# Prompt attention of a hybrid decoder: the diagonal mask moves into the scan, the heads' bias into the score products

## The chip, the cores and the metric

The kernel runs on one core of one Trainium2 chip. The metric is device time in microseconds of one execution of the whole program. Five engines work on it at the same time: TensorE (PE; its weight loads, PEld, run beside its matmuls), VectorE (DVE), ScalarE (ACT), GpSimd (POOL) and SyncE (SP), which here does nothing but issue DMAs. Each engine takes its own instructions in a fixed order and waits on semaphores for the others.

## The reference, cut to what matters

One layer of a decoder, for a prompt of 2048 tokens and a small sample group. The change touches the stick-breaking attention of the prompt alone: 8 heads of 64 channels, strictly causal.

```python
def sb_block(q, k, v, bias, q_pos, k_pos):
    z = (jnp.einsum('nqhd,nkhd->nhqk', q, k).astype(jnp.float32) * (SB_HEAD_DIM ** -0.5)
         + bias.astype(jnp.float32)[None, :, None, None])
    mask = (k_pos[None, :] < q_pos[:, None])[None, None]
    log_beta = jax.nn.log_sigmoid(z)
    log_1m = jnp.where(mask, jax.nn.log_sigmoid(-z), 0.0)
    rc = lax.cumsum(log_1m, axis=3, reverse=True)
    a = jnp.exp(jnp.where(mask, log_beta + rc - log_1m, -jnp.inf))
    return jnp.einsum('nhqk,nkhd->nqhd', a.astype(v.dtype), v)
```

For one query, the weight of key k is sigmoid(z_k) times the product of sigmoid(-z_j) over the later keys j that are still before the query. The rest of the layer (input projections, a convolution, a pooling mixer, cross-attention to a memory, the sample group's attention over a paged cache, the output projection with two norms) is as it was.

## The kernel before

The program has three stretches that follow one another on TensorE: the input projections with the sample group's paged attention beside them (to about 1486 us), the prompt's stick-breaking attention (1486 to about 1965 us), and the output projection (to the end). Everything below is about the middle one, `sb_prompt`.

**Order of the work.** The loop runs over blocks `(hp, qb)`: 4 pairs of heads, and for each 4 blocks of 512 queries. Inside a block it runs over key chunks `kc` of 512 keys from the diagonal (`kc == qb`) down to 0, and inside a chunk over 4 *steps*: query tiles `q2` = 0 and 2 (two tiles of 128 queries at a time) times the two heads `hh` of the pair. There are 40 chunks and 160 steps. TensorE's order is the order in which the program is written; the other engines' orders are set by a scheduler. A list `late` delays parts of a step: its transposes are written four steps after its scores (`TURN`), its products with the values seven steps after (`SUM` more). So while the scores of a chunk are made, the transposes belong to the chunk before it.

**One step**, with the names that the profile uses:
- `sb_scores` (L1271): 4 matmuls into `S` (PSUM, 2 buffers). Queries and keys are split into a high and a low part of fp32r. The key tile `kT` holds the high part on 64 partitions and the low part on the other 64; the query tile `Q` holds the high part (twice) and the low part (twice). Two products of depth 128 are added up.
- `sb_gates` (L1275, L1276): two sigmoids on ACT out of `S`, `gam` = sigmoid(-z) and `be` = sigmoid(z). The head's bias enters here, as an operand with one value per partition (`nbias_bc`, `bias_bc`).
- the scan (L1342 on the diagonal, L1345 else) on DVE: a running product of `gam` from the last key down, into `E`. On the diagonal it starts from 1 and `ZM` holds ones above the diagonal, so that masked keys leave the product at 1.
- the multiply (L1354) on POOL: `be` times `E`, in place.
- `turn`, four steps later: TensorE transposes the 128x128 pieces of `be` (L1373) into `AT` (PSUM, 2 buffers), three or four pieces to a tile. A full tile of 4 pieces is copied to `at` by ACT (L1378). A tile with a diagonal piece has 3 pieces (384 columns); DVE brings it out, and multiplies by a mask `tri` (L1376).
- `values`, seven steps later: products of `at` with `V`, added up in `av` (L1388). At the end of a block DVE multiplies `av` by the gate `sgt` into `sbo` (L1393), and SP stores that.

```python
                if n < 512:
                    dve.tensor_tensor(out=at[:, :n], in0=ap_[:, :n], in1=tri, op=ALU.mult)
                else:
                    act.copy(at, ap_)
```

**Loads.** `load(hp, qb)` issues 8 DMAs on SP: for each head two for `kT` (L1254) and two for `Q` (L1255). `Q` has 4 buffers, two blocks' worth, `kT` has 10. The first two blocks, (0, 0) and (0, 1), are loaded by `sb_early` before the attention stretch begins; it also makes the first two steps' scores. Side work (sums of the output weights on POOL, L1599, the end of the sample group, the head of the convolution's norm) is interleaved by step count.

Of the kernel before, what the change touches and what calls it, by code (L numbers as in the profile page):

```python
# [8 lines left out]
F32 = mybir.dt.float32  # L9
# [9 lines left out]
P = 128  # L19
# [47 lines left out]
BEB = 6  # L67
# [25 lines left out]
def kernel(  # L93
# [50 lines left out]
    mvd = dram.tile([4, P, 2, 2 * P], F32, name="mvd")  # L144
    c11d = dram.tile([8, P, 512], F32, name="c11d")
# [40 lines left out]
    nbias_bc = con.tile([P, NH], F32, name="nbias_bc")  # L186
# [250 lines left out]
    def mem_rows(mp, ps, c):  # L437
# [13 lines left out]
        if c >= 4:  # L451
            split2(mp, nat.rearrange("p t n -> p (t n)"), cc, mvd, f"v{cc}")

# [787 lines left out]
    def sb_loader(sbr):  # L1241
# [3 lines left out]
        def load(hp, qb):  # L1245
            tok = slice(512 * qb, 512 * qb + 512)
            Q = []
            for hh in range(2):
                pr = slice(64 * hh, 64 * hh + 64)
                kt = sbr.tile([P, 512], F32R, tag="kT", name=f"kT{hp}_{qb}_{hh}", bufs=10)  # L1250
                qt_ = sbr.tile([P, 2, 512], F32R, tag="Q", name=f"Q{hp}_{qb}_{hh}", bufs=4)
                for x in range(2):
                    hx = slice(64 * x, 64 * x + 64)
                    sp.dma_start(kt[hx].bitcast(F32), kd[hp, pr, x, tok])  # L1254
                    sp.dma_start(qt_[hx].bitcast(F32), qd[hp, pr, :, tok])  # L1255
                KT[hp, hh, qb] = kt
# [11 lines left out]
    def sb_scores(S, h, q2, w, Q, kt):  # L1268
        for j in range(2):
            for x in range(2):  # L1270
                pe.matmul(S[:, j, :w], lhsT=Q[:, x, P * (q2 + j) : P * (q2 + j + 1)], rhs=kt[:, :w], start=x == 0,  # L1271
                          stop=x == 1)

    def sb_gates(S, h, w, ga, be):
        act.activation(out=ga, in_=S[:, :, :w], func=AF.Sigmoid, bias=nbias_bc[:, h : h + 1], scale=-1.0)  # L1275
        act.activation(out=be, in_=S[:, :, :w], func=AF.Sigmoid, bias=bias_bc[:, h : h + 1])  # L1276

    def sb_early(load, blk, sbr, bps, early):

        room = sbr.tile([P, 16, P], F32, tag="V", name="early", bufs=2).rearrange("p (n j b) c -> p n j (b c)", n=4, j=2)  # L1280
        for n in range(2):
            blk[0, n] = load(0, n)
        for _ in range(3):
            yield
        for hh in range(2):
            S = bps.tile([P, 512], F32, tag="AT", name=f"Se{hh}", bufs=2).rearrange("p (j k) -> p j k", j=2)
            Q, KT, _ = blk[0, 0]
            sb_scores(S, hh, 0, 2 * P, Q[hh], KT[0, hh, 0])
            early[hh] = room[:, 2 * hh], room[:, 2 * hh + 1]
            sb_gates(S, hh, 2 * P, *early[hh])  # L1290
            yield

    def sb_prompt(load, loaded, sb, bps, ops, zmp, early, values_of, flags, newest):


        zm = sb.tile([P, 512], F32, tag="sbo", name="zm", bufs=1)
        pool.memset(zm, 0.0)
        pool.affine_select(out=zm[:, 384:512], in_=zm[:, 384:512], compare_op=ALU.is_gt, fill=1.0, base=0,
                           pattern=[[-1, P]], channel_multiplier=1)
        ZM = zmp.tile([P, 512], F32, name="ZM", bufs=1)  # L1300
        act.copy(ZM, zm)
        tri = sb.tile([P, 384], F32, name="tri", bufs=1)
        pool.memset(tri, 1.0)
        for c in (0, 256):
# [99 lines left out]
        for bi, (hp, qb) in enumerate(blocks):  # L1404
            if bi == 0:
                values_of(0)
# [779 lines left out]
```

## Time and profile before

| what | value |
|---|---|
| time, median of 3 runs | 2383.82 us (2381.51 to 2388.36) |
| the profiled execution's own time | 2395.19 us |
| its span, first to last instruction | 2393.5 us |
| mean granted TensorE clock | 0.987 |
| PE busy over the span | 2266.5 us |
| attention stretch, 1486 to 1970 us | PE busy 420.25, ACT 420.39, DVE 374.69, POOL 376.25 of 484 us |

Busy time is read as follows: an engine is busy from an instruction's start to its end, and overlapping instructions count once. "Idle before <- X" in a row of the profile is the idle time of the engine just before those instructions, and X is what ended it. Times of a chunk below run from the start of its first gate on ACT to the start of the next chunk's.

### The profile page before, as it was taken

How to read it: one execution, taken by the hardware profiler on the slowest of the kernel's cores; microseconds unless marked ns; L12 is line 12 of the kernel's file. 1: busy time of each engine (PE TensorE's matmuls, PEld its weight loads, DVE VectorE, ACT ScalarE, POOL GpSimd, SP SyncE). 2: the span in 40 equal slices, each digit the busy share in tenths (PEclk: the TensorE clock that was granted, in tenths of full speed). 3: DMA queues.
4: the chain of work that ended last, by engine and by line, in shares of the span. 5: the costliest groups of instructions: out<-in, count | busy, mean ns of one | idle time of the engine just before them, and what ended most of it. 6: DMA issues, size and time to landing. Idle time of an engine off the chain costs nothing. (4 is left out here: it accounts for less than half of the span.)

```text
span 2393.5 us, 43149 instructions
## 1 busy us (share of the span) xinstructions
PE 2266.5 (95%) x16512; PEld 1817.6 (76%) x16512; DVE 1686.7 (70%) x2308; ACT 1133.7 (47%) x1967; POOL 1297.7 (54%) x1348
## 2 busy tenths in 40 slices
PE   7989999999999999999999998898988889999997
PEld 7888888888888777777777776666666668787775
DVE  5332785969657674577777877878787775676997
ACT  5322243242442322224242425798989885444553
POOL 3544545555565546445556453687887773532333
PEclk9999999999999999999999999899999999999999
DMA  6678977878778999888877876564544307876774
GB/s 208 199 263 290 346 260 253 290 247 291 241 263 308 319 348 344 309 287 276 298 261 267 265 253 158 131 175 145 155 110 117 87 10 218 275 222 193 247 249 146
DMA packets 336871, 557.99 MB, mean 233 GB/s; under 512 B 27985, under 2 KB 212433, under 8 KB 320266
## 3 DMA queue, kind: packets, MB, share of 16 engines
q1 hardware_dynamic: 281290, 286.53, 39.1%
q0 software_dynamic: 55376, 268.72, 31.6%
q8 instruction: 130, 2.13, 0.4%
q14 instruction: 75, 0.61, 0.1%
HBM read 465.09 MB, written 90.68 MB: 232 GB/s over the span
## 5 line engine op out<-in xcount | busy, mean ns | idle before, releaser
L975 DVE STREAM_TRANSPOSE T<-kt 128x1024 f32<-128x1024 f32 x256 | 308.6, 1226 | 188.9 <-PE sSA L988 172.3
L942 POOL DMA_INDIRECT vt<-in_cache_v_dram,idv x256 | 252.4, 986 | 254.8 <-PE sO L1027 194.0
L627 DVE SCALAR_TENSOR_TENSOR cacc<-U,par,cacc 128x512 f32<-128x512 f32 x480 | 359.7, 749 | 11.0
L1354 POOL TENSOR_TENSOR be<-be,E 128x512 f32<-128x512 f32 (+4 forms) x316 | 301.9, 963 | 94.6 <-DVE E L1342 46.9
L1345 DVE TENSOR_TENSOR_SCAN E<-gam,cr,ZM 128x513 f32<-128x513 f32 x192 | 234.2, 1265 | 35.4 <-ACT gam L1275 30.9
L942 POOL DMA_INDIRECT kt<-in_cache_k_dram,idk x128 | 128.2, 1002 | 199.2 <-DVE T L975 156.5
L1373 PE MATMUL AT<-ident,be 128*128 128x128 f32 x1082 | 159.1, 283 | 52.5 <-DVE at L1376 36.5
L1373 PEld LDWEIGHTS AT<-ident,be 128*128 128x128 f32 x1082 | 120.3, 143 | 101.4 <-DVE at L1376 43.7
L2005 PE MATMUL acc<-wohi,mh 128*128 128x512 f32 (+1 forms) x480 | 192.3, 401 | 1.2 <-ACT mh L1729 1.1
L2005 PE MATMUL acc<-wolo,mh 128*128 128x512 f32 (+1 forms) x480 | 188.9, 393 | 0.7 <-DVE wolo L1640 0.7
L1275 ACT ACTIVATE gam<-S,nbias_bc 128x1024 f32<-128x1024 f32 (+1 forms) x158 | 170.3, 1078 | 32.1 <-PE S L1271 11.4
L1271 PE MATMUL S<-kT,Q 128*128 128x512 f32 (+1 forms) x632 | 177.1, 404 | 7.6 <-ACT be L1276 7.6
L2005 PE MATMUL acc<-wohi,ml 128*128 128x512 f32 x448 | 177.6, 396 | 6.0 <-DVE ml L1740 6.0
L1276 ACT ACTIVATE be<-S,bias_bc 128x1024 f32<-128x1024 f32 (+1 forms) x158 | 169.3, 1071 | 3.0 <-issue 3.0
L1342 DVE TENSOR_TENSOR_SCAN E<-gam,ZM 128x384 f32<-128x384 f32 (+1 forms) x124 | 96.1, 815 | 67.0 <-ACT gam L1275 66.4
L1378 ACT COPY at<-AT 128x512 f32<-128x512 f32 x224 | 126.7, 626 | 33.8 <-PE AT L1373 33.2
L988 PE MATMUL sSA<-T,W 128*32 128x128 f32 x4096 | 139.7, 276 | 2.6 <-DVE T L975 1.4
L1388 PE MATMUL av<-at,V 128*64 128x256 f32 (+1 forms) x1152 | 142.1, 389 | 0.0
L988 PEld LDWEIGHTS sSA<-T,W 128*32 128x32 f32 x4096 | 105.3, 109 | 38.0 <-issue 31.2
L1388 PEld LDWEIGHTS av<-at,V 128*64 128x64 f32 x1152 | 78.8, 142 | 60.0 <-issue 30.2
L1740 DVE TENSOR_TENSOR ml<-mr,mh 128x512 fp32r<-128x512 f32 x108 | 94.0, 878 | 42.1 <-ACT mh L1729 38.4
L1027 PE MATMUL sO<-vt,saT 128*32 128x512 f32 x1024 | 122.3, 592 | 0.0
(584 smaller groups left out, 6070.9 us busy)
## 6 DMA issues: line engine op xcount, KB each, us to landing
Q<-qd SPq DMA_DIRECT2D x64, 256.0 KB
mr<-mixd SPq DMA_DIRECT2D x32, 512.0 KB
mr<-mixd SPq DMA_DIRECT2D x48, 256.0 KB
xtp<-in_x_prompt_dram SPq DMA_DIRECT2D x16, 512.0 KB
kT<-kd SPq DMA_DIRECT2D x64, 128.0 KB
ws<-in_w_out_dram SPq DMA_DIRECT2D x16, 512.0 KB
wsd<-ws SPq DMA_DIRECT2D x16, 512.0 KB
msd<-mr SPq DMA_DIRECT2D x32, 256.0 KB
```

What stands on the lines that cost most here:

```text
L627: dve.scalar_tensor_tensor(out=ps, in0=U[:, a + k : a + k + H], scalar=wd[:, k : k + 1], in1=ps, op0=ALU.mult, op1=ALU.add)
L942: pool.indirect_dma_start(out=dst, out_offset=None, in_=rows, in_offset=bass.IndirectOffsetOnAxis(ap=idx, axis=0))
L975: S["turn"] = dve.transpose(T[:, 2 * hh : 2 * hh + 2].rearrange("p s j t -> p (s j t)"), kt[:, 2 * hh : 2 * hh + 2].rearrange("p s j d -> ...
L988: pe.matmul(sSs[n][32 * g : 32 * g + 32, P * ml : P * (ml + 1)], lhsT=W[:, jj, :], rhs=T[:, :, jj, :], start=i == 0, stop=i == 3, tile_pos ...
L1271: pe.matmul(S[:, j, :w], lhsT=Q[:, x, P * (q2 + j) : P * (q2 + j + 1)], rhs=kt[:, :w], start=x == 0, stop=x == 1)
L1275: act.activation(out=ga, in_=S[:, :, :w], func=AF.Sigmoid, bias=nbias_bc[:, h : h + 1], scale=-1.0)
L1276: act.activation(out=be, in_=S[:, :, :w], func=AF.Sigmoid, bias=bias_bc[:, h : h + 1])
L1345: dve.tensor_tensor_scan(out=E[:, j][:, ::-1], data0=g_[:, j][:, ::-1], data1=ZM[:, 0:1].to_broadcast([P, 513]), initial=carry[hh, q2][:, ...
L1354: newest.append(pool.tensor_tensor(out=be[:, j, :m], in0=be[:, j, :m], in1=E[:, j, 513 - w : 513 - w + m], op=ALU.mult).ins)
L1373: pe.transpose(ap_[:, n : n + P], A[hp, qb, kc, hh, qt][:, P * r : P * (r + 1)], ident)
L1388: pe.matmul(av[64 * hh : 64 * hh + 64, c], lhsT=V[:, 4 * kc + r, 64 * hh : 64 * hh + 64], rhs=ats.pop((hp, qb, kc, hh, q2, r)), start=dg a ...
L2005: pe.matmul(o[:rows], lhsT=m[a][:, k, :rows], rhs=W[prod, 4 * h + k][w], start=not cont and h == k == n == 0, stop=h == 1 and k == 3 and n ...
```

## The change

1. **Mask in the scan.** On the diagonal the scan starts from 0 instead of 1, and `ZM` has a single 1 at the query's own key. Coming down from the last key, `E` stays 0 over the masked keys, becomes 1 at the own key, and is the running product below it. So `be` times `E` is masked already. The multiply leaves out the last column of the tile; a new POOL memset of two elements per partition (one per query tile) sets that column of `be` to 0. `tri` is gone, and every tile of transposes, whole or of 384 columns, is copied by ACT.
2. **Bias in the products.** Keys now have two tiles: `kh` with the high part on both halves, and `kl` with the low part on 64 partitions and the head's bias (high and low part) on two more. `Q`'s first half holds the query's high part over its low part, its second half the high part and two rows of ones. The scores are one product of depth 128 and one of depth 66; that leaves out low times low. `sb_gates` has no bias operand any more. The bias rows are made once, in the projections (`bias_rows`), and stored in `bd`.
3. **Loads.** 16 DMAs for a block instead of 8 (two of them 2 rows, for each head). The keys have a tag for each `qb`: 4 buffers for `qb` = 0, 2 for the others, which lie in the pool that opens with the attention stretch. So `sb_early` loads block (0, 0) alone, and (0, 1) is loaded at the start of the attention. Each later block's load is written at the start of the block before, as it was.
4. **Memory.** The gated result is written in place over `sgt` (one buffer) and stored from there, so the next gate's load waits for that store; before, it waited for the multiply. `be` has 5 buffers instead of 6.

```diff
-                kt = sbr.tile([P, 512], F32R, tag="kT", name=f"kT{hp}_{qb}_{hh}", bufs=10)
+                kts = [(sbr if qb == 0 else KT["pool"]).tile([P, 512], F32R, tag=f"k{n}{qb}", name=f"k{n}{hp}_{qb}_{hh}",
+                                                             bufs=2 if qb else 4) for n in "hl"]
                 qt_ = sbr.tile([P, 2, 512], F32R, tag="Q", name=f"Q{hp}_{qb}_{hh}", bufs=4)
                 for x in range(2):
                     hx = slice(64 * x, 64 * x + 64)
-                    sp.dma_start(kt[hx].bitcast(F32), kd[hp, pr, x, tok])
-                    sp.dma_start(qt_[hx].bitcast(F32), qd[hp, pr, :, tok])
-                KT[hp, hh, qb] = kt
+                    sp.dma_start(kts[0][hx].bitcast(F32), kd[hp, pr, 0, tok])
+                    sp.dma_start(qt_[hx, 0].bitcast(F32), qd[hp, pr, x, tok])
+                sp.dma_start(kts[1][:64].bitcast(F32), kd[hp, pr, 1, tok])
+                sp.dma_start(qt_[:64, 1].bitcast(F32), qd[hp, pr, 0, tok])
+                sp.dma_start(kts[1][64:66].bitcast(F32), bd[2 * hp + hh])
+                sp.dma_start(qt_[64:66, 1].bitcast(F32), bd[NH])
+                KT[hp, hh, qb] = kts
...
+    def sb_scores(S, q2, w, Q, kts):
         for j in range(2):
-            for x in range(2):
-                pe.matmul(S[:, j, :w], lhsT=Q[:, x, P * (q2 + j) : P * (q2 + j + 1)], rhs=kt[:, :w], start=x == 0,
-                          stop=x == 1)
+            c = slice(P * (q2 + j), P * (q2 + j + 1))
+            pe.matmul(S[:, j, :w], lhsT=Q[:, 0, c], rhs=kts[0][:, :w], start=True, stop=False)
+            pe.matmul(S[:, j, :w], lhsT=Q[:66, 1, c], rhs=kts[1][:66, :w], start=False, stop=True)
...
-        act.activation(out=ga, in_=S[:, :, :w], func=AF.Sigmoid, bias=nbias_bc[:, h : h + 1], scale=-1.0)
-        act.activation(out=be, in_=S[:, :, :w], func=AF.Sigmoid, bias=bias_bc[:, h : h + 1])
+        act.activation(out=ga, in_=S[:, :, :w], func=AF.Sigmoid, scale=-1.0)
+        act.activation(out=be, in_=S[:, :, :w], func=AF.Sigmoid)
...
-        for n in range(2):
-            blk[0, n] = load(0, n)
-        for _ in range(3):
+        blk[0, 0] = load(0, 0)
+        for _ in range(4):
             yield
...
+                if dg:
+                    own = be.rearrange("p j k -> p (j k)")
+                    step_ = be.shape[2] + P
+                    pool.memset(own[:, w - P - 1 : w + step_ - P : step_], 0.0)
...
-                                               data1=ZM[:, 512 - n : 512][:, ::-1], initial=1.0, op0=ALU.mult, op1=ALU.max)
+                                               data1=ZM[:, 512 - n : 512][:, ::-1], initial=0.0, op0=ALU.mult, op1=ALU.max)
...
-                if n < 512:
-                    dve.tensor_tensor(out=at[:, :n], in0=ap_[:, :n], in1=tri, op=ALU.mult)
-                else:
-                    act.copy(at, ap_)
+                act.copy(at[:, :n], ap_[:, :n])
...
-                mo = sb.tile([P, 512], F32, tag="sbo", name=f"sbo{hp}_{qb}", bufs=1)
-                dve.tensor_tensor(out=mo, in0=av, in1=gt, op=ALU.mult)
-                (pool if (hp, qb) == blocks[-1] else sp).dma_start(mix_rows(8 + hp, 512 * qb, 512), by_tile(mo))
+                dve.tensor_tensor(out=gt, in0=av, in1=gt, op=ALU.mult)
+                (pool if (hp, qb) == blocks[-1] else sp).dma_start(mix_rows(8 + hp, 512 * qb, 512), by_tile(gt))
...
+            if bi + 1 < len(blocks):
+                loaded[blocks[bi + 1]] = load(*blocks[bi + 1])
             if bi == 0:
                 values_of(0)
-            if bi + 1 < len(blocks) and blocks[bi + 1] not in loaded:
-                loaded[blocks[bi + 1]] = load(*blocks[bi + 1])
```

Names in the rows below are tile, then `hp_qb_kc_hh_q2` (for `kh`, `Q` and `av`: `hp_qb...`), then a serial number.

DVE before, where the second half of block (1, 1)'s chunk 0 passes into block (1, 2): two masked tiles of the diagonal chunk (1, 1, 1) stand between the scans of later steps.

```order
L1345 SCALAR_TENSOR_TENSOR E1_1_0_0_2_16550<-gam0_14876,cr1_1_1_0_2_16427,ZM_14870 128x513
L1376 TENSOR_TENSOR at1_1_1_0_2_1_16491<-AT1_1_1_0_2_1_16490,tri_14872 128x384
L1345 SCALAR_TENSOR_TENSOR E1_1_0_0_2_16550<-gam0_14876,cr1_1_1_0_2_16427,ZM_14870 128x513
L1345 SCALAR_TENSOR_TENSOR E1_1_0_1_2_16578<-gam1_14878,cr1_1_1_1_2_16448,ZM_14870 128x513 x2
L1376 TENSOR_TENSOR at1_1_1_1_2_1_16523<-AT1_1_1_1_2_1_16522,tri_14872 128x384
L1342 SCALAR_TENSOR_TENSOR E1_2_2_0_0_16613<-gam2_14880,ZM_14870 128x128
```

The same place on DVE in the changed kernel:

```order
L1363 SCALAR_TENSOR_TENSOR E1_1_0_1_0_16597<-gam2_14881,cr1_1_1_1_0_16484,ZM_14875 128x513 x2
L1363 SCALAR_TENSOR_TENSOR E1_1_0_0_2_16652<-gam0_14877,cr1_1_1_0_2_16519,ZM_14875 128x513 x2
L1363 SCALAR_TENSOR_TENSOR E1_1_0_1_2_16680<-gam1_14879,cr1_1_1_1_2_16541,ZM_14875 128x513 x2
L1360 SCALAR_TENSOR_TENSOR E1_2_2_0_0_16715<-gam2_14881,ZM_14875 128x128
L1360 SCALAR_TENSOR_TENSOR E1_2_2_0_0_16715<-gam2_14881,ZM_14875 128x256
```

The masked tiles are gone from DVE, and the scans stand one behind the other.

ACT before, in the chunk behind a diagonal one (block (1, 2), chunk 1): gates of the four steps, and the two full tiles of the diagonal chunk.

```order
L1275 ACTIVATE gam0_14876<-S1_2_1_0_0_16673,nbias_bc_119 128x2x512
L1276 ACTIVATE be1_2_1_0_0_16678<-S1_2_1_0_0_16673,bias_bc_118 128x1024
L1275 ACTIVATE gam1_14878<-S1_2_1_1_0_16698,nbias_bc_119 128x2x512
L1276 ACTIVATE be1_2_1_1_0_16703<-S1_2_1_1_0_16698,bias_bc_118 128x1024
L1275 ACTIVATE gam2_14880<-S1_2_1_0_2_16730,nbias_bc_119 128x2x512
L1276 ACTIVATE be1_2_1_0_2_16735<-S1_2_1_0_2_16730,bias_bc_118 128x1024
L1378 COPY at1_2_2_0_2_0_16747<-AT1_2_2_0_2_0_16746 128x512
```

ACT now, the same steps:

```order
L1295 ACTIVATE gam0_14877<-S1_2_1_0_0_16777 128x2x512
L1296 ACTIVATE be1_2_1_0_0_16782<-S1_2_1_0_0_16777 128x1024
L1393 COPY at1_2_2_0_0_0_16794<-AT1_2_2_0_0_0_16793 128x384
L1295 ACTIVATE gam1_14879<-S1_2_1_1_0_16803 128x2x512
L1296 ACTIVATE be1_2_1_1_0_16808<-S1_2_1_1_0_16803 128x1024
L1393 COPY at1_2_2_1_0_0_16830<-AT1_2_2_1_0_0_16829 128x384
L1295 ACTIVATE gam2_14881<-S1_2_1_0_2_16835 128x2x512
L1296 ACTIVATE be1_2_1_0_2_16840<-S1_2_1_0_2_16835 128x1024
L1393 COPY at1_2_2_0_2_0_16852<-AT1_2_2_0_2_0_16851 128x512
L1393 COPY at1_2_2_0_2_1_16859<-AT1_2_2_0_2_1_16858 128x384
```

Each step of the diagonal chunk has a copy of 384 columns on ACT now, between the gates of later steps, and the gates read `S` alone.

SP before, where the projections end (`ydw`, `gsd`: their last stores; `V0`: the first values): the loads of block (0, 1) stand ahead of all of these, and the next ones are for block (0, 2).

```order
L1254 DMA kT0_1_1_14713<-kd_58 64x512
L1255 DMA Q0_1_1_14714<-qd_57 64x2x512
L729 DMA gsd_61<-sg1sg3_0_14731 128x512
L729 DMA gcd_60<-sg1cg3_1_14771 128x512
L549 DMA mixd_63<-mo1_3_512_14784 128x4x128
L634 DMA ydw_62<-acc1_3_1_14847 128x512
L1264 DMA V0_14882<-vd_59 128x16x128
L729 DMA gsd_61<-sg1sg3_1_14828 128x512
L1254 DMA kT0_2_0_14912<-kd_58 64x512
```

SP now, from the last `ydw` store on:

```order
L649 DMA ydw_62<-acc1_3_1_14854 128x512
L1271 DMA Q0_1_0_14885<-qd_57 64x512
L1273 DMA Q0_1_0_14885<-qd_57 64x512
L1275 DMA Q0_1_0_14885<-bd_69 2x512
L1271 DMA Q0_1_1_14896<-qd_57 64x512 x2
L1273 DMA Q0_1_1_14896<-qd_57 64x512
L1275 DMA Q0_1_1_14896<-bd_69 2x512
L744 DMA gsd_61<-sg1sg3_1_14828 128x512
L1284 DMA V0_14905<-vd_59 128x16x128
L1270 DMA kh0_1_0_14883<-kd_58 64x512 x2
L1272 DMA kl0_1_0_14884<-kd_58 64x512
L1274 DMA kl0_1_0_14884<-bd_69 2x512
```

The keys of block (0, 1) are issued behind the last stores and the first values now, twelve and more DMAs later than `ydw`.

More of the change, by code (lines that the diff above doesn't have):

```diff
@@ L66 @@
 SUM = 3
-BEB = 6
+BEB = 5
 ATB = 6
@@ L452, in mem_rows, with bias_rows @@
             split2(mp, nat.rearrange("p t n -> p (t n)"), cc, mvd, f"v{cc}")
+    def bias_rows():
+        b = zc.tile([NH, 1], F32, name="brow")
+        sp.dma_start(b, sb_bias.rearrange("o h -> h o"))
+        hl = zc.tile([NH, 2], F32R, name="bhl")
+        t = k4("brows", [P, 2, 512], F32)
+        pool.memset(t[: NH + 1], 1.0)
+        for _ in range(3):
+            yield
+        dve.tensor_copy(hl[:, 0:1], b)
+        dve.tensor_tensor(out=hl[:, 1:2], in0=b, in1=hl[:, 0:1].bitcast(F32), op=ALU.subtract)
+        for x in range(2):
+            dve.tensor_copy(t[:NH, x], hl[:, x : x + 1].bitcast(F32).to_broadcast([NH, 512]))
+        sp.dma_start(bd, t[: NH + 1])
     def half_rows(j):
@@ L1882 @@
         sp.dma_start(bias_bc, sb_bias[0].partition_broadcast(P))
-        dve.tensor_scalar(out=nbias_bc, in0=bias_bc, scalar1=-1.0, scalar2=None, op0=ALU.mult)
+        tasks.add(bias_rows())
         tasks.add(params)
```

28 lines of the change are left out of this document (11 added, 17 removed).

## The prediction

> **What bounds the kernel now.** The windows view came first, cut where TensorE changes its work (length, then busy us of PE, PEld, DVE, ACT and POOL, then the granted clock):
>
> ```profile
> 0.00:1486.31 1486.31, 1453.14 (x11781) 1200.34 (x11782) 993.61 (x1382) 505.38 (x948) 776.00 (x746) 1.00 0.81 274
> 1486.31:1609.24 122.93, 102.47 (x674) 73.21 (x673) 96.35 (x118) 101.53 (x135) 89.99 (x122) 0.92 0.59 156
> 1609.24:1726.05 116.81, 103.95 (x721) 74.16 (x721) 92.00 (x101) 103.28 (x137) 95.56 (x120) 0.99 0.54 154
> 1726.05:1846.51 120.46, 105.89 (x725) 75.39 (x726) 92.52 (x101) 106.38 (x144) 97.34 (x120) 0.97 0.44 121
> 1846.51:1965.00 118.49, 103.72 (x708) 73.55 (x707) 91.36 (x103) 105.42 (x144) 90.03 (x116) 0.97 0.22 55
> 1965.00:2393.50 428.50, 397.31 (x1910) 320.91 (x1910) 320.86 (x506) 211.75 (x466) 148.82 (x128) 0.98 0.67 216
> ```
>
> The first and last rows are the projections: PE is busy 98% and 93% of them, and the change leaves their work alone. The four rows between are the attention, one row for each `hp`. There nobody is the bound: PE is busy 88%, ACT 87%, DVE and POOL under 82%. So the waits decide. They come next, from the groups of instructions within 1486 to 1970 us:
>
> ```profile
> L1373 PE MATMUL AT<-ident,be 128*128 128x128 f32 x1058 | 155.9, 283 | 52.5 <-DVE at L1376 36.5 <-ACT at L1378 13.0 <-POOL be L1354 1.2
> L1376 DVE TENSOR_TENSOR at<-AT,tri 128x384 f32<-128x384 f32 x64 | 34.2, 539 | 0.4 <-PE AT L1373 0.3
> ```
>
> Of PE's 63 us of idle time in the stretch, 36.5 end when DVE has multiplied a diagonal tile by `tri`. The multiply itself takes 0.54 us; the timeline around 1640 us shows what it stands behind:
>
> ```profile
> 1638.75 3.62 DVE L1345 TENSOR_TENSOR_SCAN E<-gam,cr,ZM 128x513 f32<-128x513 f32 x3
> ...
> 1642.28 0.53 DVE L1376 TENSOR_TENSOR at<-AT,tri 128x384 f32<-128x384 f32 x1
> ...
> 1642.87 0.73 PE L1373 MATMUL AT<-ident,be 128*128 128x128 f32 x4 [2.40 <-DVE at L1376]
> ...
> 1643.64 0.59 ACT L1378 COPY at<-AT 128x512 f32<-128x512 f32 x1 [1.90 <-PE AT L1373]
> ...
> 1644.39 2.87 PE L1388 MATMUL av<-at,V 128*64 128x256 f32 x16
> ...
> 1650.94 1.95 PE L1388 MATMUL av<-at,V 128*64 128x256 f32 x16
> ```
>
> Three scans (3.62 us) go first; PE, with both `AT` buffers full, idles 2.40 us, and then ACT 1.90 us, because the scores that feed its gates are queued on PE behind those transposes. Then PE is slow as well: the same 16 value products take 2.87 us instead of 1.95, at a granted clock of 0.50:
>
> ```profile
> 1644.00:1646.00 2.00, 2.00 (x11) 1.17 (x11) 0.66 (x2) 1.49 (x3) 1.68 (x5) 0.50 0.98 363
> ```
>
> Last, the ten chunks of `hp` = 1, in order (0,0); (1,1), (1,0); (2,2), (2,1), (2,0); (3,3), (3,2), (3,1), (3,0), named by `qb` and `kc`:
>
> ```profile
> 1609.24:1620.52 11.28, 10.69 (x82) 8.06 (x83) 6.66 (x9) 10.59 (x17) 6.95 (x10) 1.00 0.86 253
> 1620.52:1630.09 9.57, 8.82 (x61) 6.10 (x60) 8.03 (x13) 7.59 (x12) 7.52 (x13) 1.00 0.91 243
> 1630.09:1639.99 9.90, 8.82 (x62) 6.18 (x62) 9.90 (x13) 9.23 (x10) 9.38 (x10) 1.00 0.37 113
> 1639.99:1655.15 15.16, 12.62 (x82) 8.98 (x82) 8.48 (x12) 10.57 (x16) 9.37 (x14) 0.89 0.60 187
> 1655.15:1665.55 10.40, 9.32 (x63) 6.46 (x62) 10.03 (x12) 9.30 (x11) 9.18 (x12) 1.00 0.18 53
> 1665.55:1679.15 13.60, 10.94 (x82) 7.95 (x81) 11.35 (x11) 12.28 (x16) 12.85 (x15) 1.00 0.43 134
> 1679.15:1690.28 11.13, 11.00 (x82) 8.05 (x81) 6.51 (x9) 10.45 (x17) 7.63 (x13) 1.00 0.67 167
> 1690.28:1700.70 10.42, 9.34 (x63) 6.47 (x63) 10.05 (x12) 9.30 (x12) 9.59 (x12) 1.00 0.26 75
> 1700.70:1714.26 13.56, 11.38 (x82) 8.09 (x81) 11.32 (x11) 12.17 (x17) 12.09 (x17) 1.00 0.69 216
> 1714.26:1726.05 11.79, 11.04 (x81) 7.82 (x79) 9.67 (x9) 11.79 (x17) 11.00 (x12) 1.00 0.34 78
> ```
>
> Chunks that no `tri` multiply falls into run at their busiest engine: (3,3) takes 11.13 with PE busy 11.00, (3,0) 11.79 with ACT busy 11.79. Chunks behind a diagonal one, such as (1,0) and (3,2), run at DVE's pace (9.90 of 9.90, 10.05 of 10.42). And three run far over every engine, just after the multiplies: (2,2), (2,0) and (3,1).
>
> **The change, part by part.**
>
> *ACT gains copies.* 64 tiles of 384 columns move to it. A copy of that shape, and two of 512 back to back:
>
> ```profile
> L713 ACT COPY zt0v<-z0v x12: 387/479/482, 173.7 to 234.7; 128x384 f32<-128x384 f32 x8, 128x288 f32<-128x288 f32 x4
> ...
> 1671.93 1.08 ACT L1378 COPY at<-AT 128x512 f32<-128x512 f32 x2
> ```
>
> One of 512 lasts 0.59 alone (1643.64), so a second adds 0.49: neighbours overlap by 0.10. A copy of 384 costs 0.48 - 0.10 = 0.38 in a row of work: 64 x 0.38 = +24 us, 0.48 each (+31) where it stands alone.
>
> *ACT's gates lose their bias operand.* No gate without one is in the trace, but a sigmoid of the same shape out of PSUM is, between two biased ones:
>
> ```profile
> 1488.04 0.71 ACT L1276 ACTIVATE early<-Se,bias_bc 128x512 f32<-128x512 f32 x1
> ...
> 1488.61 0.62 ACT L717 ACTIVATE sg1sg<-z1sg 128x512 f32<-128x512 f32 x1
> 1489.09 1.15 ACT L1275 ACTIVATE gam<-S,nbias_bc 128x1024 f32<-128x1024 f32 x1
> ```
>
> From start to start the biased one takes 0.57, the other 0.48. I take 0.09 for each of 320 gates: -29 us. Bounds: nothing (the operand is free and the difference has another reason), and 0.17 (54 us), the difference of these means:
>
> ```profile
> L1275 ACT ACTIVATE gam<-S,nbias_bc 128x512 f32<-128x512 f32 x30 | 23.3, 775 | 2.5 <-ACT at L1378 1.3 <-PE S L1271 0.6 <-DVE E L1342 0.3
> L717 ACT ACTIVATE sg1sg<-z1sg 128x512 f32<-128x512 f32 x8 | 4.8, 602 | 7.1 <-PE z1sg L251 5.2 <-issue 1.9
> ```
>
> 0.09 is the one from neighbouring rows. So ACT comes out even over the stretch (+24 - 29), but not everywhere: a chunk behind a diagonal one gets 4 x 0.38 - 8 x 0.09 = +0.8, every other one -0.7.
>
> *DVE loses* 64 x 0.54 = 34 us of multiplies, and with them PE's 36.5 us of waiting. Chunk by chunk for `hp` = 1, by the busiest engine that is left:
> - (2,2): no stall and no slow clock, so as (3,3): 15.16 to 11.1, -4.0.
> - (2,0): ACT 12.28 - 0.7 = 11.6, but POOL was busy 12.85 with side work; 12.4, -1.2. (3,1): ACT 11.5, POOL 12.1; 12.0, -1.6.
> - (3,0): ACT 11.1, PE 11.0; 11.4 with a little left over, -0.4.
> - (1,0), (2,1), (3,2): DVE falls to about 7.9, ACT rises to 10.0 to 10.1; 10.2 each: +0.3, -0.2, -0.2. DVE's pace is exchanged for ACT's here.
> - (1,1): -0.2. (0,0), (3,3): PE's, -0.1 together.
>
> That makes -7.6. The other three `hp` have the same chunks; their rows above are 120.46, 118.49 and 122.93. I take -8, -8 and, for `hp` = 0 without its start, -6.
>
> Half of (2,2)'s gain hangs on the clock. The Trainium skill ("TensorE: Matmul & The Clock Gate", section "HAM oscillation — how this bites in real kernels") says that only idle gaps over about 3.4 us cool the array to half its clock. Here a gap of 2.40 us already did, by the row at 1644 us. By the page (2,2) would win the 2.4 us stall alone, and the four of them 6 us less; the sum goes by the row.
>
> *PE* does the same number of matmuls over the same columns. A product of depth 66 has no row here. Nearest are products of 512 columns on other operands:
>
> ```profile
> L2005 PE MATMUL acc<-wolo,mh 128*128 128x512 f32 (+1 forms) x480 | 188.9, 393 | 0.7 <-DVE wolo L1640 0.7
> L1271 PE MATMUL S<-kT,Q 128*128 128x512 f32 (+1 forms) x632 | 177.1, 404 | 7.6 <-ACT be L1276 7.6
> ```
>
> Their means differ by 0.011 us, or 3.5 us on the 320 products concerned; I take no gain and no loss, with that as the bound either way.
>
> *POOL* gains 64 memsets of two elements, ahead of the multiply that already waits for the scan:
>
> ```profile
> L1310 POOL MEMSET gam<- x3: 91/91/92, 1488.1 to 1488.1; 128x2 f32 x3
> ```
>
> 64 x 0.09 = 6 us at most, hidden where POOL waits for DVE; in (2,0), where POOL is full, it is within the 12.4. Five buffers of `be` cost nothing: the step that takes a buffer over, five steps later, has its scores behind the old step's transposes on PE anyway. The load of `sgt` waits for a store instead of a multiply; it is needed a chunk later at the least, after block (hp, 0), some 10 us, so nothing, unless SP is blocked for most of that. Behind it on SP stand the next block's loads. `bias_rows` is a few small instructions in a stretch where PE is 98% busy: nothing.
>
> *SP* issues 8 more DMAs for each of 16 blocks:
>
> ```profile
> L1254 SPq DMA_DIRECT2D kT<-kd x64: 444/588/1913, 1469.8 to 1829.2; - x64
> ```
>
> At 0.59 that is 76 us of queue in 484. A block's `Q` can be fetched when the last scores of two blocks before are done; after a change of `hp` that leaves block (hp, 0), 11.28 us, for 8 issues (4.7 us) and a landing: covered, with 4 us to spare if SP is free. Not covered is the start. The keys of (0,1) now go behind the `ydw` store (just ahead of `V` at 1486.98), 7 loads of `Q`, `gsd` and `V`:
>
> ```profile
> 1486.98 0.92 SPq L1264 DMA_DIRECT2D V<-vd  x1
> ...
> 1491.82 0.73 PE L1271 MATMUL S<-kT,Q 128*128 128x256 f32 x4 [3.55 <-ACT be L1276]
> ...
> 1496.98 1.22 PE L1271 MATMUL S<-kT,Q 128*128 128x256 f32 x4 [4.01 <-ACT be L1276]
> ...
> 1480.00:1500.00 20.00, 12.44 (x58) 10.07 (x57) 14.77 (x24) 10.48 (x15) 8.71 (x20) 0.83 1.03 252
> ```
>
> Thirteen issues at 0.59, 7.7 us, end at 1494 to 1495; `Q`, `V` and one head's keys, 2.2 MB, take 8.6 us at the 252 GB/s of that window, so they are there at about 1497 to 1499. Before, the first scores of (0,1) ran at 1491.82, the second only at 1496.98. I take +4, with bounds 0 (the second scores were late anyway) and +8.
>
> *Sum*: -7.6 - 8 - 8 - 6 + 4 = -25.6, say -26 us. Against the profiled execution's own 2395.2 us that is 2369; the median of the runs shown, 2383.8, lies 11.4 us under that execution, so 2358 us.
>
> **Rivals.**
> 1. *PE alone becomes the bound.* If every other wait goes too, the four rows shrink to PE's busy time, 416 of 478.7 us: -63 + 4, so 2325 us. For it: ACT comes out even while its waits on PE vanish. Against: ACT is as full as PE in (3,0) and stays so.
> 2. *The wait only changes its name.* The copy stands behind two gates on ACT (2 x 1.0 us) as the multiply stood behind scans, and PE waits 36 us for "ACT at". 2384, give or take 7 us (0.3%, about what the runs can tell from no change). Against: PE runs these transposes before the scores of the next gates, so ACT's gates are done when it gets the tile.
> 3. *ACT becomes the bound, and it is slower.* If the operand is free (bound 0) and each copy costs 0.48, the chunks behind a diagonal one get 1.9 us more of ACT: (1,0) to 11.1, (2,1) and (3,2) to 11.2, +2.8 for each `hp`. With the waits of rival 2 and the start, +11 + 4: 2399 us. It decides where the operand is worth under 0.04 us.
>
> **How the numbers follow.** The forecast's case (-12 to -45, so 2339 to 2372) gets 0.67, rival 1 0.08, rival 2 0.13, rival 3 0.12, for it or another wait of the kind, late keys above all. Faster by over 0.3% is the first two, 0.75; within 0.3% 0.13; slower 0.12. The likeliest time is 2358 us; its own range is 2339 to 2372. From 2336 to 2386 takes in that and most of rival 2 and leaves out about 2 in 10.
>
> **What would show it.** Right: no "DVE at" before L1391's transposes, and under 20 us of "ACT at"; the chunk (2,2) at about 11 us with clock 1.00; gates of 1024 columns about 0.09 shorter than the means of 1149 and 1142 ns in the page; scores of (0,1) at about 1498. Wrong: gates as long as before; PE waiting for `Q` or `kh` after each change of `hp`; POOL's `be` ending most of the transposes' waits, since POOL has no slack in (2,0) and (3,1).

## The result, and the profile after

The changed kernel takes 2350.93 us (median of 4 runs, 2347.41 to 2353.95), the kernel before 2382.66 (4 runs, 2378.83 to 2388.36): the ratio is 0.9864, 95% interval 0.984 to 0.9889, or 32 us less. Forecast were 2358 us and a range of 2336 to 2386.

First the windows view of the changed kernel, cut at the same events as before: the projections, the four `hp` of the attention (start of the first gate to start of the next `hp`'s), the rest. The columns are length, then busy us of PE, PEld, DVE, ACT and POOL, the granted clock, DMA share and GB/s.

```profile
0.00:1479.69 1479.69, 1449.00 (x11781) 1199.11 (x11781) 992.45 (x1385) 505.39 (x948) 774.56 (x737) 1.00 0.81 275
1479.69:1596.63 116.94, 97.86 (x676) 71.90 (x675) 89.36 (x102) 99.44 (x151) 90.68 (x145) 0.91 0.63 172
1596.63:1702.25 105.62, 100.73 (x722) 73.56 (x722) 84.40 (x85) 101.21 (x153) 96.12 (x136) 1.00 0.61 176
1702.25:1810.56 108.31, 101.38 (x723) 73.66 (x723) 84.63 (x85) 103.92 (x159) 97.90 (x137) 1.00 0.48 134
1810.56:1919.70 109.14, 100.14 (x709) 72.05 (x707) 83.84 (x87) 103.51 (x161) 90.27 (x132) 1.00 0.21 56
1919.70:2348.10 428.40, 397.79 (x1914) 322.00 (x1910) 320.00 (x507) 211.87 (x466) 147.09 (x128) 0.98 0.66 216
```

From `hp` = 1 on PE is busy 92 to 95% and ACT 95 to 96% of the time, at a granted clock of 1.00. From the first gate to the last copy into `at`, the attention took 495.4 us before and takes 456.8, 38.7 less. The first row holds more than it shows; see "The bias rows" below.

The groups of instructions within the attention, 1480 to 1950 us:

```profile
L1391 PE MATMUL AT<-ident,be 128*128 128x128 f32 x1082 | 150.0, 278 | 24.3 <-ACT at L1393 17.9 <-POOL be L1372 3.6 <-DVE cy L1481 0.4
L1291 PE MATMUL S<-kh,Q 128*128 128x512 f32 x256 | 113.1, 442 | 0.0
L1292 PE MATMUL S<-kl,Q 66*128 66x512 f32 x256 | 102.4, 400 | 0.0
L1295 ACT ACTIVATE gam<-S 128x1024 f32<-128x1024 f32 x128 | 140.1, 1094 | 8.4 <-PE S L1292 5.1 <-issue 1.9 <-ACT at L1393 0.9
L1393 ACT COPY at<-AT 128x384 f32<-128x384 f32 x64 | 34.6, 541 | 1.5 <-PE AT L1391 1.5
```

The transposes' wait for "DVE at" (36.5 us before) is gone; "ACT at" ends 17.9 us of idle time against 13.0. Gates of 1024 columns last 1094 ns instead of 1149, and back to back `be` starts 0.917 us after `gam` instead of 1.011.

The chunk (2,2) of `hp` = 1 and the two others that ran far over every engine, (2,0) and (3,1), in the windows view:

```profile
1626.86:1637.68 10.82, 10.82 (x82) 8.32 (x83) 7.08 (x10) 9.87 (x17) 9.31 (x18) 1.00 0.70 231
...
1647.63:1658.79 11.16, 10.93 (x81) 8.03 (x82) 9.73 (x9) 11.16 (x17) 11.16 (x13) 1.00 0.26 97
...
1679.72:1691.06 11.34, 11.34 (x82) 8.33 (x83) 10.27 (x10) 11.34 (x18) 11.34 (x16) 1.00 0.55 168
```

They fell from 15.16, 13.60 and 13.56 us, and now run at PE's, ACT's and POOL's pace. The start got worse, as the timeline shows:

```profile
1485.18 4.15 SPq L1270 DMA_DIRECT2D kh<-kd  x2
...
1490.03 0.43 SPq L1274 DMA_DIRECT2D kl<-bd  x1
...
1494.92 0.55 PE L1291 MATMUL S<-kh,Q 128*128 128x256 f32 x1 [13.18 <-DMA kh<-kd]
```

PE idles 13.18 us for the keys of (0,1), and the first chunk takes 16.63 us instead of 10.51.

### The profile page after: what moved, and what is told of

Same layout as the page of the kernel before. It is cut to its first block, busy times and chain, and to the rows that moved or that the text cites. A ratio compares the mean times of both kernels' runs of the same rounds, so it can differ in the third digit from the quotient of the medians.

```text
span 2348.1 us, 43432 instructions
## 1 busy us (share of the span) xinstructions
PE 2246.9 (96%) x16512; PEld 1812.3 (77%) x16512; DVE 1654.7 (70%) x2247; ACT 1125.3 (48%) x2031; POOL 1296.6 (55%) x1410
## 5 line engine op out<-in xcount | busy, mean ns | idle before, releaser
L1391 PE MATMUL AT<-ident,be 128*128 128x128 f32 x1082 | 150.0, 278 | 24.3 <-ACT at L1393 17.9
L1295 ACT ACTIVATE gam<-S 128x1024 f32<-128x1024 f32 (+1 forms) x158 | 162.4, 1028 | 17.7 <-PE S L1292 14.3
L1393 ACT COPY at<-AT 128x512 f32<-128x512 f32 (+1 forms) x288 | 161.3, 647 | 18.7 <-PE AT L1391 18.6
L1296 ACT ACTIVATE be<-S 128x1024 f32<-128x1024 f32 (+1 forms) x158 | 161.6, 1023 | 0.0
L1291 PE MATMUL S<-kh,Q 128*128 128x512 f32 (+1 forms) x316 | 132.0, 422 | 13.2 <-DMA kh<-kd 13.2
L1403 PE MATMUL av<-at,V 128*64 128x256 f32 (+1 forms) x1152 | 136.3, 377 | 0.0
```

What stands on the lines that cost most here:

```text
L1295: act.activation(out=ga, in_=S[:, :, :w], func=AF.Sigmoid, scale=-1.0)
L1296: act.activation(out=be, in_=S[:, :, :w], func=AF.Sigmoid)
L1391: pe.transpose(ap_[:, n : n + P], A[hp, qb, kc, hh, qt][:, P * r : P * (r + 1)], ident)
L1393: act.copy(at[:, :n], ap_[:, :n])
L1403: pe.matmul(av[64 * hh : 64 * hh + 64, c], lhsT=V[:, 4 * kc + r, 64 * hh : 64 * hh + 64], rhs=ats.pop((hp, qb, kc, hh, q2, r)), start=dg a ...
```

## The experiments

Three questions: which half of the change makes the gain, what the half that did not look like a gain costs, and what can be mended. The table has the duration of `hp` = 1's chunks in each profile (us, start of the first gate to the next chunk's first gate; "behind" is the sum of (1,0), (2,1), (3,2)).

| kernel | (2,2) | (2,0) | (3,1) | behind | all ten | `hp` = 0's first chunk | whole attention |
|---|---|---|---|---|---|---|---|
| before | 15.16 | 13.60 | 13.56 | 30.73 | 116.8 | 10.51 | 495.4 |
| before, second profile | 14.96 | 13.54 | 15.18 | 30.74 | 118.2 | 10.60 | 493.8 |
| no operand, no bias | 16.19 | 12.05 | 12.13 | 32.68 | 115.4 | 9.05 | 478.1 |
| bias part only | 13.36 | 12.03 | 12.14 | 32.66 | 112.6 | 16.34 | 480.8 |
| changed, 384 columns by DVE | 13.34 | 12.05 | 12.16 | 32.65 | 112.6 | 16.18 | 481.1 |
| mask part only | 11.15 | 11.79 | 11.80 | 31.24 | 110.6 | 9.46 | 471.4 |
| changed, operand back | 11.16 | 11.80 | 11.79 | 31.23 | 110.7 | 15.66 | 475.8 |
| changed | 10.82 | 11.17 | 11.34 | 29.77 | 105.6 | 16.63 | 456.8 |

### One half at a time

*The mask part alone*, on the kernel before: `ZM`, the start from 0, the memset and ACT's copies, as in the diff of the change.

> The kernel before with the mask half of the change alone: the scan starts from 0 with a 1 at the own key, two elements of be are set to 0, ACT copies every tile. The gates keep their bias operand, keys and queries are loaded as before. Theory (both halves are needed: the mask takes DVE's stalls away, the missing operand pays for ACT's copies): TensorE no longer waits for DVE's at, but ACT has 320 x 0.094 = 30 us more than in the changed kernel. Where ACT sets the pace there (the three chunks behind a diagonal one, (2,0), (3,1) and (3,0): 24 of 40 chunks) that is 8 x 0.094 = 0.75 us each, 18 us; the late start (6 us) is not there. So 2351 + 18 - 6 = 2363, a gain of 20 of the 32 us. Rival 1 (the mask makes it all, ACT has room anyway): 2345. Rival 2 (the wait only changes its name, to ACT's at, once ACT is full): 2384, with 30 us or more of TensorE idle before the transposes on ACT's at.

Measured: 2359.12 us against 2379.94, ratio 0.9903 (0.9882 to 0.9924), a gain of 21 us. The groups of this kernel:

```profile
L1275 ACT ACTIVATE gam<-S,nbias_bc 128x1024 f32<-128x1024 f32 (+1 forms) x158 | 187.2, 1185 | 8.2 <-PE S L1271 5.0 <-issue 2.5 <-ACT at L1373 0.6
...
L1371 PE MATMUL AT<-ident,be 128*128 128x128 f32 x1082 | 153.6, 280 | 39.8 <-ACT at L1373 34.9 <-POOL be L1352 2.7 <-DVE cy L1462 0.3
```

So PE's waits before the transposes go from 36.5 us of "DVE at" and 13.0 of "ACT at" to 34.9 of "ACT at" and none of "DVE at". The name did change, as rival 2 had it, and yet two thirds of the gain are there: the waits are 51 of 0.68 us on average, where "DVE at" had 27 of 1.35, and no half-clock window lies in `hp` = 1 or 2 any more. Theory and number hold; rivals 1 and 2 of the expectation fall.

*The bias part alone*: the changed kernel with the mask part taken back.

```diff
-                                               data1=ZM[:, 512 - n : 512][:, ::-1], initial=0.0, op0=ALU.mult, op1=ALU.max)
+                                               data1=ZM[:, 512 - n : 512][:, ::-1], initial=1.0, op0=ALU.mult, op1=ALU.max)
...
-                act.copy(at[:, :n], ap_[:, :n])
+                if n < 512:
+                    dve.tensor_tensor(out=at[:, :n], in0=ap_[:, :n], in1=tri, op=ALU.mult)
+                else:
+                    act.copy(at, ap_)
```

> The changed kernel with the mask half undone: the scan starts from 1, DVE multiplies the diagonal tiles by tri (kept in bf16, and cr with 8 buffers, for room), no elements set to 0. Products of depth 66, gates without operand and the new loads stay. Theory (both halves needed): the stalls on DVE's at stay, about 35 us of TensorE idle, with the granted clock near 0.50 behind the one in chunk (2,2); ACT's 30 us less count only where it set the pace in the kernel before, (2,0), (3,1), (3,0): 12 x 0.75 = -9 us, and the start costs +6. So about 2380. Rival (the missing operand makes most of the gain, since a fuller ACT was what kept be and at late): 2360 or less.

Measured: 2376.53 us against 2379.94, ratio 0.9986 (0.9972 to 0.9999): 3 us. The stalls stayed:

```profile
L1393 PE MATMUL AT<-ident,be 128*128 128x128 f32 x1058 | 155.0, 281 | 42.1 <-DVE at L1396 35.3 <-ACT at L1398 5.6 <-DVE cy L1486 0.4
```

One thing came out other than expected: the chunks behind a diagonal one got 0.64 us longer each (32.66 for the three against 30.73). With ACT quicker, the wait for DVE's tile falls into them: PE's waits for it in (2,1) and (3,2) of `hp` = 1 grow from 0.8 to 2.0 us each, and in (2,0) and (3,1) they shrink from 2.1 to 0.9.

*The place or the multiply?* The changed kernel again, with only this:

```diff
-                act.copy(at[:, :n], ap_[:, :n])
+                if n < 512:
+                    dve.tensor_copy(at[:, :n], ap_[:, :n])
+                else:
+                    act.copy(at, ap_)
```

> The changed kernel, but the tiles of 384 columns are brought out by a plain copy on DVE, in the place where the multiply by tri stood; the mask stays in the scan. It tells whether the multiply or its place behind DVE's scans cost the time. Theory (the place: three scans go first): as bias_only, 2376, with 30 us or more of TensorE idle on DVE's at and chunks (2,2), (2,0) and (3,1) of hp = 1 at 13.4, 12.0 and 12.1 us. Rival (the multiply by a second operand was the cost, or the scans' start from 1): as the changed kernel, 2348, less what ACT wins.

Measured: 2380.25 us against 2384.35, ratio 0.9991 (0.9975 to 1.0008), and chunk for chunk the times of the bias part alone, within 0.02 us in the table's columns of `hp` = 1.

```profile
L1391 PE MATMUL AT<-ident,be 128*128 128x128 f32 x1058 | 154.7, 281 | 42.0 <-DVE at L1394 35.0 <-ACT at L1396 5.3 <-DVE cy L1484 0.4
L1394 DVE COPY at<-AT 128x384 f32<-128x384 f32 x64 | 34.2, 539 | 0.7 <-PE AT L1391 0.5
```

A mask in the scan that leaves the copy on DVE is worth nothing that these runs can tell. So it is not the multiply: a plain copy takes DVE the same 539 ns. What paid is that the tile is no longer brought out by DVE. PE's 32 waits for it are 1.09 us long on average, twice the copy itself, so a good part of them is the queue behind the scans; the runs do not separate that from DVE's 34 us of copying.

### The price of the operand

The changed kernel with an operand of zeros on its gates:

```diff
-        act.activation(out=ga, in_=S[:, :, :w], func=AF.Sigmoid, scale=-1.0)
-        act.activation(out=be, in_=S[:, :, :w], func=AF.Sigmoid)
+        act.activation(out=ga, in_=S[:, :, :w], func=AF.Sigmoid, bias=zero_[:, 0:1], scale=-1.0)
+        act.activation(out=be, in_=S[:, :, :w], func=AF.Sigmoid, bias=zero_[:, 1:2])
```

> The changed kernel, with a bias operand on the gates again that holds zeros: nothing but the price of the operand. Theory: each gate starts 0.094 us later after the one before it, as in the traces (1.011 and 0.997 us from start to start with it, 0.917 and 0.905 without): 30 us of ACT, of which 24 of the 40 chunks pay 0.75 us, +18: 2369. If ACT is the bound everywhere, +30: 2381. If the operand is not what made the gates shorter, 2351 and gates as long as in the changed kernel.

Measured: 2374.94 us against 2379.94, ratio 0.9975 (0.9959 to 0.9991). The changed kernel's own ratio, taken in other runs, would be 2347.6 on that before, so by the times the operand costs about 27 us, but the intervals of the two ratios leave some 7 us open either way. The profiles say less: the attention differs by 19.0 us, and the ten chunks of `hp` = 1 by 5.0 and those of `hp` = 2 by 5.4, where the expectation's 18 would make 4.5 and ACT's whole 30 would make 7.5. That is near the 18 expected. The gates start 1.009 us after one another again:

```profile
L1297 ACT ACTIVATE gam<-S,zero__120 128x1024 f32<-128x1024 f32 x128 | 160.2, 1252 | 7.0 <-PE S L1294 4.9 <-issue 1.4 <-ACT at L1395 0.7
```

The mean of one is 1252 ns here, 1094 without and 1149 in the kernel before, although the start to start is the same 1.009 to 1.011 in the first and the last: the length of an overlapped instruction is not its price.

This run settles a second thing. Chunk by chunk its times for `hp` = 1 are those of the mask part alone (110.7 and 110.6; for `hp` = 2 both take 113.7), although it has the products of depth 66, the doubled loads and five buffers of `be`: in these chunks those cost nothing and save nothing.

The operand in the kernel before, with the bias left out of the scores:

> The kernel before with its gates' bias operand left out, the bias itself too (no bias enters the scores): the operand's price alone, without the new loads, the late start, the product of depth 66 or the mask. Theory: as bias_only without its start: 6 us under it, 2370, a gain of about 10 of the 32 us; DVE's at keeps TensorE waiting as long as before. Chunks (2,0), (3,1), (3,0) shrink, those behind a diagonal chunk don't, since DVE sets their pace. Rival 1 (the operand is free where DVE is late): 2380. Rival 2 (products of depth 66 or the new loads cost or save something of their own): the chunks of hp = 1 come out other than in bias_only by over 0.3 us each.

Measured: 2366.92 us against 2384.35, ratio 0.993 (0.9909 to 0.9952): a gain of 17 us where 10 to 14 had been worked out. All but one chunk of `hp` = 1 agree with the bias part alone within 0.04 us; (2,2) is 16.19 against 13.36, with the same stall and two half-clock windows more (below). The operand is thus worth 17 us while DVE's stalls are there, and 19 (profiles) to 27 (times) once they are gone.

In the profiles the changed kernel's attention, late start included, is 38.7 us shorter than before (37.0 against the second profile of the kernel before), and the whole gained 32: some 5 to 7 us are missing.

### The bias rows

They are found in the projections, which the prediction had end as before. The time at which PE starts its 400th instruction says otherwise: 77.1, 75.1, 75.0 and 76.2 us in the four profiles without those rows (two of the kernel before, the mask part alone, and no operand with no bias), 83.1 to 84.3 in the first six with them. SP's part of the timeline in the changed kernel, then in the second profile of the kernel before:

```profile
71.59 0.28 SPq L467 DMA_DIRECT2D bd<-brows  x1
71.97 0.34 SPq L492 DMA_DIRECT2D ht<-in_state_pool_dram  x1
...
75.35 1.03 PE L510 MATMUL hps<-ident,ht 120*128 120x120 f32 x4 [6.40 <-DMA ht<-in_state_pool_dram]
```

```profile
63.71 0.39 SPq L477 DMA_DIRECT2D ht<-in_state_pool_dram  x1
```

The store of the rows waits on SP for DVE, which gets to them at 70.82, and the load of `ht` stands behind it; it leaves 8.3 us later, and PE idles 6.40 us for it. Two kernels test this, and a third below. The rows later, their store three steps after they are made:

```diff
-        tasks.add(bias_rows())
         tasks.add(params)
...
         for _ in range(3):
             tasks.step()
+        tasks.add(bias_rows())
...
+        for _ in range(3):
+            yield
         sp.dma_start(bd, t[: NH + 1])
```

> The changed kernel with the bias rows made later in the projections (after the histories of the sample group have been loaded), and their store written three steps after they are made. In every profile with the bias rows TensorE runs 7 to 9 us later from its 400th instruction on (83.1 to 84.3 us against 75.0 to 77.1 without), with 6.4 us of waiting for the load of ht, which stands on SP behind the store of bd. Theory (that store's wait for DVE blocks SP, and this costs the change 8 us of the whole time): 8 us under the changed kernel, 2343, and the 400th instruction at 75 to 77 us. Rival (the 8 us are given back, or come from the rows wherever they are made): 2351.

And the kernel before, with `bias_rows` and `bd` and nothing else of the change:

> The kernel before, with the bias rows made and stored where the change makes them, and used by nobody: their price alone. Theory: +8 us, 2391, all of it between 45 and 85 us. Rival (the lateness comes from other parts of the change, and the rows are free): 2383.

Measured: the changed kernel with late rows 2343.58 us against 2381.16, ratio 0.9846 (0.9826 to 0.9866). That is 7 us better than the change as it was made by the medians and 4 by the ratios, whose intervals overlap, so the time alone does not show it; the profile does, with the 400th instruction at 75.2 us. The rows alone 2393.34, ratio 1.0051 (1.0034 to 1.0067), 12 us slower and clear of noise, 400th instruction at 84.0; the profile shows 7 to 9 us there, and the rest of the 12 was not traced. The theory holds: the rows alone bring the lateness, and moving their store takes it away.

```profile
63.75 0.39 SPq L494 DMA_DIRECT2D ht<-in_state_pool_dram  x1
```

(The late rows: the load leaves when it did before.)

### The start, and both mended

The keys of (0,1) before the attention, in the buffers of the `qb` = 0 keys that are idle until `hp` = 1:

```diff
-                kts = [(sbr if qb == 0 else KT["pool"]).tile([P, 512], F32R, tag=f"k{n}{qb}", name=f"k{n}{hp}_{qb}_{hh}",
-                                                             bufs=2 if qb else 4) for n in "hl"]
+                first = qb == 0 or (hp, qb) == (0, 1)
+                kt_tag = "ab"[(hp + qb) % 2] if first else qb
+                kts = [(sbr if first else KT["pool"]).tile([P, 512], F32R, tag=f"k{n}{kt_tag}", name=f"k{n}{hp}_{qb}_{hh}",
+                                                           bufs=2) for n in "hl"]
...
-        blk[0, 0] = load(0, 0)
+        for n in range(2):
+            blk[0, n] = load(0, n)
...
-            if bi + 1 < len(blocks):
+            if bi + 1 < len(blocks) and blocks[bi + 1] not in loaded:
```

> The changed kernel with the keys of block (0,1) loaded before the attention stretch again: they take the two pairs of buffers of the qb = 0 keys that lie idle until hp = 1, so no memory is added; the keys of (1,0) then wait for them. Theory: TensorE's 13.2 us wait for kh near 1482 to 1495 goes, chunk (0,0) of hp = 0 falls from 16.6 to about 10.5 us, -6: 2345, with no new wait of TensorE for kh or Q at the change to hp = 1 (the last scores with the old keys are made a whole chunk, 11 us, before). Rival 1: the wait moves to V or to the keys at the change of hp, and nothing is gained: 2351. Rival 2: SP, blocked by the wait of (1,0)'s keys, delays stores and gates, +3 or more.

Measured: 2343.36 us against 2379.94, ratio 0.9835 (0.9811 to 0.9859): 7 us better than the change, though the intervals of the two ratios overlap a little; in the profiles the attention is 9.9 us shorter. The scores now wait for ACT, not for a load, and no wait for `kh` or `Q` stands at a change of `hp`:

```profile
1485.93 0.39 PE L1293 MATMUL S<-kh,Q 128*128 128x256 f32 x1 [3.60 <-ACT be L1298]
```

The first chunk takes 7.30 us instead of 16.63, less than the 10.5 expected. Both mended at once:

> The changed kernel with both mended: the keys of (0,1) loaded before the attention, and the bias rows later. The two gains lie in different stretches, so theory: they add up, -7 and -8: 2336. Rival (one of them gives way to another wait): 2343 or more.

Measured: 2335.76 us against 2381.16, ratio 0.9813 (0.9794 to 0.9831). Against the change's 0.9864 (0.984 to 0.9889) that is some 12 us, clear of noise: the two gains add up as far as these runs can tell, and this is the fastest kernel of the study, 45 us under the kernel before.

### Two small ones

> The changed kernel without POOL's 64 memsets, so the last masked element of each diagonal row stays in the weights: the price of the memsets alone. Theory: 64 x 0.1 = 6 us of POOL are hidden, except perhaps in (3,1), where POOL is busy 11.34 of 11.34 us: 2348, within 3 us of the changed kernel. Rival (POOL is the pace in the chunks with side work): -6, 2342.

Measured: 2353.12 us against 2384.35, ratio 0.9876 (0.9851 to 0.99), the changed kernel's within the intervals; its chunks of `hp` = 1 take 105.6 us with and without them. The memsets cost nothing that these runs can tell.

> The kernel before once more, unchanged, for a second profile: the first one's own time lay 11.4 us over the median of the runs shown. If the surplus lies in the projections, they end some 6 us earlier than at 1486 us and the attention takes 490 to 495 us again; if it lies in the attention, that takes 484 to 488 us.

Measured: 2380.78 us, one run. Its attention takes 493.8 us, the first profile's 495.4: the surplus lay in the projections. PE starts its 800th and 1000th instruction at 136.0 and 161.3 us here, at 137.6 and 170.8 in the first profile; PE waits there for ACT's copy into `zt0k`, in the groups of 138 to 171 us of the first profile:

```profile
L379 PE MATMUL nt0k<-ident,zt0k 128*128 128x128 f32 x16 | 3.0, 294 | 6.6 <-ACT zt0k L701 6.6
```

In the second profile it is 0.8 us. So it was nothing of the attention's, and making the sum against that execution's own time was right.

## Why the prediction was right, and which steps were not

The forecast lay 7 us over the measured time, which is inside its range. The mechanism was right. That the sum came so near is partly luck: the attention gained 38.7 us where the terms made 25.6, and the bias rows, put at nothing, took 6.5 to 8.5 of that back. By its terms, from the profiles:

| term | forecast | profile after against before |
|---|---|---|
| `hp` = 1's ten chunks | -7.6 | -11.2 |
| `hp` = 2, 3 | -8, -8 | -12.2, -9.3 |
| `hp` = 0 without its first chunk | -6 | -12.1 |
| start | +4 | +6.1 |
| `bias_rows` (in the projections; against both profiles of before) | 0 | +6.5 to +8.5 |

- **DVE's stalls vanish** (-36.5 us of waits): right, and shown to come from bringing the tile out on DVE at all, not from the multiply.
- **The operand, 0.09 us for each gate**: right (0.094 and 0.092 from start to start). The sign that the forecast named for it, means shorter by about 0.09, is not what came: they fell by 0.055 and 0.052, since means of overlapped instructions don't show the price. That its saving is to pay for the copies was right too: with the operand left in, the mask part gains 21 of the 32.
- **Copies of 384, 0.38 us in a row**: right (0.371 median from start to start).
- **(2,2) 15.16 to 11.1**: 10.82, clock 1.00. Half of it hung on the clock: where a like stall (2.05 us) cools nothing, the chunk takes 13.34 to 13.36 us, so at most 1.8 of the 4.3 us are the clock's (the stall was 2.40 us before).
- **(2,0) to 12.4, (3,1) to 12.0, "POOL was busy 12.85 with side work"**: the step that was mis-sized most within `hp` = 1; 11.17 and 11.34. Busy time in a stalled chunk is not that chunk's work. The groups of POOL's instructions in (2,0), before, then after:

```profile
L1354 POOL TENSOR_TENSOR be<-be,E 128x512 f32<-128x512 f32 x11 | 11.8, 1091 | 0.7 <-ACT at L1378 0.7
L1599 POOL TENSOR_TENSOR ws<-ws,ws 128x512 f32<-128x512 f32 x2 | 2.5, 1275 | 0.0
```

```profile
L1372 POOL TENSOR_TENSOR be<-be,E 128x512 f32<-128x512 f32 x9 | 9.6, 1084 | 0.0
L1613 POOL TENSOR_TENSOR ws<-ws,ws 128x512 f32<-128x512 f32 x2 | 2.5, 1271 | 0.0
```

  A chunk owns 8 multiplies; the stalled one also worked off what was late. Eight at about 1.06 us from start to start, two sums at 1.25 and the copies of `cr` make 11.3, which is what came.
- **Chunks behind a diagonal one, +0.3, -0.2, -0.2**: 0.00, -0.46, -0.50. ACT's count from start to start is 8 x 0.911 + 4 x 0.371 + 2 x 0.467 = 9.7 us, and they take 9.9; the forecast took its 10.1 from ACT's busy time, again with the overlaps and late work of a stalled run in it.
- **`hp` = 0, -6, and `hp` = 2, -8**: the largest misses, and no chunk of theirs had been worked out. The forecast counted the clock in the chunks (2,2) alone. Time at half clock fell from 16.8 to 7.9 us in `hp` = 0 (its first chunk left out) and from 6.8 to 0 in `hp` = 2; in the second profile of the kernel before it was 15.3 and 3.4, so a part of these two terms differs from one execution to the next.
- **PE busy 88%**: 416 of 478.7 us are 87%, as much as ACT; nothing in the sum hangs on it.
- **Depth 66, no gain and no loss**: right by the run with the operand back, and by the products' means: 442 and 400 ns now, 422 for both before.
- **Start, +4**: +6.1. Thirteen issues to the end of the first head's keys were put at 7.7 us; from the first `Q` (1480.19) they took 10.3, 4.15 of it for the two behind the load of `V`, and the keys were there 4.5 us later.
- **"`bias_rows` is a few small instructions ...: nothing"**: wrong, and the step that failed. The instructions are cheap; the store waits on SP, and what stands behind it was not asked, although the forecast asked just that for the store of `sgt`.
- **Rival 1** fell: PE is busy 92 to 95% from `hp` = 1 on, and ACT is as full. **Rival 2** fell by its price: where the gates keep their operand its wait does come ("ACT at" 34.9 us), and yet the time falls by 21 us; in the change it is 17.9. **Rival 3** fell by its own test twice: the operand costs 0.094 us, and even with it the chunks behind a diagonal one take 10.41, not 11.1, and the kernel gains.

## What to carry to other kernels

Bring a result out on an engine whose queue is short at that moment: the same copy on DVE, behind three scans, gave the whole gain back. Work out what a chunk needs by counting its own instructions from start to start; busy time in a stretch with stalls contains the work that was late. And for every new small DMA, list what stands behind it on its queue and when its input is ready: one store of a few rows made PE 7 to 9 us late, out of 45 us that were to be had.

## What the runs showed of the hardware

PE's clock falls on a fixed grid. In each profile all half-clock stretches within the attention begin on one grid of 3.413 us and last one period or several. The windows view of the kernel before, cut on that grid, twice two periods, each around the same kind of stall, 2.08 us:

```profile
1581.88:1585.29 3.41, 1.33 (x11) 1.00 (x10) 3.41 (x4) 2.60 (x3) 3.41 (x6) 1.00 0.74 202
1585.29:1588.70 3.41, 3.41 (x13) 1.85 (x14) 2.08 (x3) 2.15 (x3) 3.03 (x4) 0.50 0.94 326
1663.80:1667.21 3.41, 1.91 (x11) 1.45 (x11) 3.41 (x4) 2.77 (x4) 3.41 (x5) 1.00 0.00 0
1667.21:1670.62 3.41, 2.64 (x18) 1.84 (x20) 3.08 (x4) 2.47 (x4) 3.41 (x5) 1.00 0.00 0
```

```profile
1584.72 0.66 PE L1373 MATMUL AT<-ident,be 128*128 128x128 f32 x4 [2.08 <-DVE at L1376]
1667.98 0.66 PE L1373 MATMUL AT<-ident,be 128*128 128x128 f32 x4 [2.08 <-DVE at L1376]
```

The first stall lies in one period (PE busy 1.33 of 3.41 us), and the next runs at half clock; the second is cut by the grid, and no period is cooled. Over the 13 profiles of this study, 1498 to 1915 us, that makes 1529 periods that began warm. All 23 with PE idle for 1.95 us or more in sum (transposes counted as busy) were followed by half clock, 7 of 18 with 1.6 to 1.95, and 6 of 1488 with less (all near 1524 to 1541 us, not explained). So whether a stall of 2 us costs the clock too hangs on where the grid falls, and it changes a chunk by some 1.6 us from one execution to the next: (3,1) of `hp` = 1 took 13.56 and 15.18 us in the two profiles of the kernel before. The Trainium skill ("TensorE: Matmul & The Clock Gate", section "What's actually happening") describes such a free-running window of 3413 ns, and the traces agree; its section on oscillation asks for idle gaps over about 3.4 us, and there the measurement decides: 1.95 us within one window were enough.

Whether more is to be had from PE's remaining waits was not tried. In (2,0), (3,1) and (3,0) of the changed kernel PE, ACT and POOL are all within 0.3 us of the chunk's length.
